# A small scale tile allocated ahead of the split norm operands: their start moves from 0 to 32 modulo 64 bytes

## The chip, the core and the metric

The kernel runs on one core of a Trainium2 chip. The metric is the device time of one execution, in microseconds (us); it is given as the median of several runs. The engines are TensorE (PE; its weight loads are shown apart as PEld), VectorE (DVE), ScalarE (ACT), GpSimd (POOL) and the DMA queue that SyncE issues (SP).

## What is computed

One decoder layer on 512 tokens of width 1024, in float32: a first feed-forward block, two token mixers side by side (a sparse attention whose keys an indexer selects, and a gated linear recurrence) that are merged through gates, a second feed-forward block, and a gated embedding block. Every block stands between two RMS norms.

```python
def reference(x, p, ...):
    h = x
    h = h + 0.5 * rms_norm(swiglu(rms_norm(h, ffn1_pre_g), w_gate, w_up, w_down), ffn1_post_g)   # width 2816 inside
    proj = rms_norm(h, mix_pre_g) @ w_in           # q, latents, index queries and keys, q/f/i/g of the recurrence, gates
    y_a = dsa_branch(...)                          # index scores, top 128 keys per query, attention of 8 heads
    y_b = rms_norm(hgrn2_chunkwise(...), hgrn_norm_g) * silu(g_h)
    merged = sigmoid(gate_a + b) * (y_a @ w_br_a) + sigmoid(gate_b + b) * (y_b @ w_br_b)
    h = h + rms_norm(merged @ w_out, mix_post_g)
    h = h + 0.5 * rms_norm(swiglu(rms_norm(h, ffn2_pre_g), ...), ffn2_post_g)
    return h + rms_norm(sigmoid(rms_norm(h, ple_pre_g) @ w_ple_gate) * (p @ w_ple_proj), ple_post_g)
```

## The kernel before

Activations lie feature-major: a tile of 128 partitions holds 128 features, and 512 tokens run along the free dimension; 1024 features are eight such tiles (index k). A product is made of three matmuls for each step of the contraction, because both operands are split into a high and a low part of a reduced float32 type: weight high by data high, weight low by data high, weight high by data low (`mm3_step`, the matmul of line 239). So a product of 1024 features and 512 tokens is 24 matmuls of 512 columns.

The split data lie in three pairs of tiles:

- `hg_hi` and `hg_lo`, [128, 8, 512] each: h times the gain of the next norm, in parts. They are written by ScalarE (line 283) and VectorE (line 284), and are the data of the gate and up products of both feed-forward blocks, of nearly all of the mixers' products, and of the last block's. In the merge they hold the two branches' results. Where a result is wanted token-major (the values, lines 623 to 625; the latents; the last block) they are the stationary operand and the weight is the moving one.
- `hid_hi` and `hid_lo`: the hidden layer of a feed-forward block, the data of its down products.
- `m_hi` and `m_lo`: the merged branches, the data of w_out's product.

A weight comes by DMA into one of three `raw` tiles, 512 KB at a time, is split by ScalarE (line 163) and VectorE or GpSimd (line 165) into one of six `w` tiles, and is then the stationary operand. `R` holds the norm's scale per token, spread over the partitions; it is multiplied onto a product when VectorE takes it out of PSUM (`scaled`, line 360). `r`, [128, 4], holds the same scale with one token per partition.

Outside the mixers the program's text sets the order, block by block, and at a block's end the last product runs in halves of the tokens (256 columns) beside the norms. In the mixers a table (`PLAN`) says which steps of the scores, the selection, the attention and the recurrence go out behind each product. Each engine takes its instructions in order.

Where tiles lie is settled by the order of allocation. The pools const, keep, wpool and tmp are stacked, and every tile is rounded up to 32 bytes of a partition. `hg_hi`, `hg_lo`, `R` and `r` are the four tiles of keep, in that order, allocated at the end of `consts` (lines 130 to 133). `r` is 16 bytes long and takes 32, so all that follows keep begins 32 bytes past a multiple of 64.

Of the kernel before, what the change touches and what calls it, by code (L numbers as in the profile page):

```python
# [14 lines left out]
P = 128  # L15
# [31 lines left out]
BANKS = {"mm": 2, "pl": 2, "hg": 2, "pt": 1, "po": 1}  # L47
# where a block ends: how many tiles of its last product run in halves of the tokens; for each half, how many matrix
# products go out at the most before the norm's two steps, and how many of the residual's tiles GpSimd adds
TURN = {  # L50
# [3 lines left out]
}  # L54
# the first weights of a block, with * for those whose low part GpSimd takes
FIRST = {"mix": "---*", "ffn2": "*---", "proj": "---", "ple": "-*--*--*"}
# the products of the mixers in order, and the steps of the scores, of the selection, of the attention and of the
# recurrence that go out behind each; * for a product whose weight's low part GpSimd takes
PLAN = (
# [11 lines left out]
class Layer:  # L71
# [27 lines left out]
    def consts(self):  # L99
# [28 lines left out]
        nc.vector.tensor_scalar_add(self.lbn, self.lb, -1.0)  # L128

        self.hg_hi = self.keep.tile([P, KT, NT], F32R, name="hg_hi")  # L130
        self.hg_lo = self.keep.tile([P, KT, NT], F32R, name="hg_lo")
        self.R = self.keep.tile([P, NT], F32, name="R")
        self.r = self.keep.tile([P, 4], F32, name="r")

    def bias_vector(self):
        """The relative bias less its last bucket's, over the scale, for the distances 255 to -128; each head's
        vector is laid out P times, so that a read with rows of BVEC - 1 shifts it by one each."""
        nc, c = self.nc, self.const
        onehot = self.t(BVEC)[:32]
        nc.sync.dma_start(onehot, self.a["onehot"])  # L140
        rel = c.tile([32, HEADS], F32, name="rel")
        nc.sync.dma_start(rel, self.a["rel_bias"])
        far = c.tile([HEADS, 1], F32, name="far")
        nc.sync.dma_start(far, self.a["rel_far"])
        ps = self.bank("pl")
        nc.tensor.matmul(ps[:HEADS, :BVEC], rel, onehot, start=True, stop=True)
        bv = self.t(BVEC)[:HEADS]
        nc.vector.tensor_scalar(bv, ps[:HEADS, :BVEC], far, 1.0 / ATT_SCALE, op0=OP.subtract, op1=OP.mult)
        nc.sync.dma_start(self.bias_d, bv.unsqueeze(1).to_broadcast([HEADS, P, BVEC]))
# [21 lines left out]
    def first_weights(self, name, srcs, n, own=()):  # L171
        """The first weights of a block, the last of them in tiles of the block's own."""
        own = [None] * (len(srcs) - len(own)) + list(own)
        flags = self.first[name]
        return [self.weight(src, n, w, self.nc.gpsimd if next(flags) == "*" else None) for src, w in zip(srcs, own)]

    def weight(self, src, n, w=None, eng=None):
        """One group of a weight: [128, n] raw to its high and low parts."""
        raw = self.raw_tile()
# [9 lines left out]
    def bank(self, tag=None):  # L189
        """A bank of PSUM; outside the mixers the products go round all but those of the norms."""  # L190
        if tag is None:
# [3 lines left out]
    def mm3(self, ps, w, hi, lo, n, cols, c0=0):  # L195
        """ps = w^T x over n tiles of the contraction, from the parts of both."""
        self.mm3s([(ps, w)], hi, lo, n, cols, c0)

    def mm3s(self, outs, hi, lo, n, cols, c0=0):
        """The same for several pairs of a result and a weight, side by side along the contraction."""  # L200
        for k in range(n):
# [21 lines left out]
    def power(self, out, ss, n, *ds):  # L223
        """out = (ss/d + eps)^-1/2"""
        nc = self.nc
# [6 lines left out]
    def issue_after(self, later, earlier):  # L232
        """An order of two instructions of one engine."""
        self.tc.add_manual_dep(later.ins, earlier.ins.name, mybir.DependencyInfo(
            mybir.DependencyClass.NoSync, mybir.DependencyReason.DATA), reason="order of issue")

    def matmul(self, *args, **kw):
        """A product of the main stream, after the ones that ask to go ahead of it."""
        i = self.nc.tensor.matmul(*args, **kw)  # L239
# [7 lines left out]
    def rms(self, acc, cols, r, spread=True, waits=None):  # L247
        """r[token] = (sum(acc)/D + eps)^-1/2 for the tokens of cols; returns it spread over a PSUM tile."""
        nc = self.nc
# [17 lines left out]
    def square_sum(self, acc, src, first, eng):  # L267
        """acc (+)= src^2"""
        nc = self.nc
# [9 lines left out]
    def prenorm_tile(self, k, gname, acc, cols):  # L279
        """h[k] times its gain, in parts; its squares go to acc."""  # L280
        nc = self.nc
# [13 lines left out]
    def start(self, *srcs):  # L295
        """The input and its norm's operands, with the first weights between them; returns the weights."""
        nc = self.nc
# [27 lines left out]
    def residual(self, y, acc, g, nxt, turn, spill=None):  # L325
        """For each half of the tokens: h += g * y / rms(y), and the next norm's operands."""
        nc = self.nc
# [16 lines left out]
    def last_product(self, product, y, acc, g, nxt, turn, spill=None):  # L344
        """The last product of a block: its second half of the tokens runs beside the first half's norms."""
        split = KT - turn[0]
# [10 lines left out]
    def scaled(self, ps, cols=FULL):  # L357
        """The norm's scale on a product, feature-major."""
        t = self.t(cols.stop - cols.start)
# [68 lines left out]

# [1 line left out]

# [19 lines left out]
    def kv_product(self, k, ps, i, ws):  # L450
        """Step k of the contraction of the latents, the index keys and the index weights of token tile i."""
        tok = slice(i * P, (i + 1) * P)
# [6 lines left out]
    def kv_tile(self, i, ps):  # L459
        """Tokens of tile i: the normed latents and index keys, and the index weights, token-major."""  # L460
        nc = self.nc
# [25 lines left out]
    def stacked(self, q, o, t0):  # L487
        """The queries from token t0 of one head of a pair: the high part and the low part, on half of the partitions each."""
        nc = self.nc
# [7 lines left out]
    def dots(self, m, q):  # L497
        """The index scores of heads 2m and 2m + 1, added for the query tiles past the first. A head's queries are
        stacked in both parts on the partitions, so that one pass takes them against one part of the keys."""
        nc = self.nc  # L500
# [21 lines left out]
    def topk(self, qt):  # L522
        """Each query's scores to a mask: 0 for its best TOPK keys, MASKED for the others."""
        nc = self.nc
# [10 lines left out]
    def attention(self, hd):  # L535
        """A head over its own keys, which lie on the partitions twice, against its queries in both parts."""
        nc = self.nc
# [49 lines left out]
    def head_keys(self, m):  # L587
        """The keys of the heads 2m and 2m + 1 from the latents."""
        nc = self.nc
# [15 lines left out]
    def head_values(self):  # L605
        """The values of all heads from the latents, token-major."""
        nc = self.nc
# [23 lines left out]
    def forget(self, ps, hd):  # L631
        """k = 1 - f, and the sums of log f from the start of each chunk."""
        nc = self.nc
# [153 lines left out]
    def mixers(self):  # L787
# [58 lines left out]
        for step, n_dots, n_top, n_att, n_hg in PLAN:  # L846
# [19 lines left out]
            for j, (g, n) in enumerate(((dots, n_dots), (top, n_top), (att, n_att), (hg, n_hg))):  # L866
                run(g, n)
                done[j] += n
            # a query tile's selection comes after all scores, and before its attention
            assert done[0] >= 8 or not done[1]  # L870
# [10 lines left out]
    def merge(self, pool):  # L881
        """The two branches through their gates, w_out, and the residual."""
        nc, a = self.nc, self.a
# [17 lines left out]

        # the first branch runs ahead, for it is ready before the other
        for i in range(KT + LEAD):
# [23 lines left out]
    def ple_proj(self, pool):  # L927
        """The other product of the last block, token-major, which waits for nothing: it fills the end of the first block."""
        nc, a = self.nc, self.a
# [12 lines left out]
    def tok_mm3s(self, outs, w, hi, lo):  # L942
        """For each of several results, some columns of a token tile of x^T w."""
        n = len(w)
# [7 lines left out]
    def ple(self, pp, y, pool):  # L952
        """The last block, token-major: its norm's sums lie along the rows, and a token tile ends by itself."""
        nc, a = self.nc, self.a
# [80 lines left out]
def _square(w, m_tiles):  # L1035
    """[K, M] to [M/128, 128, K]: for each tile of columns, all of the contraction with 128 rows a step."""
    k, m = w.shape
# [63 lines left out]
```

## Time and profile before

| | |
|---|---|
| median of 3 runs | 1270.4 us (1266.41 to 1270.44) |
| span of the profiled execution | 1267.0 us (no other time of it is recorded) |
| PE busy | 1246.2 us, 98% |
| VectorE, ScalarE, GpSimd busy | 56%, 42%, 23% |
| matmuls in the trace | 6263 |
| granted TensorE clock | full but for single slices |

PE's busy time counts matmuls that overlap, so the length of one matmul is no measure of its cost. What one adds is the distance from its start to the next one's start; it is read from the timeline, or from a piece of the chain of work that ended last, where so many matmuls in a row take so long.

### The profile page before, as it was taken

The page shows a single profiled execution, that of the slowest core. Times are in us where ns is not written, and L with a number is a line of the kernel's source. Part 1 is how long each engine was busy: PE and PEld are TensorE (multiplying, and loading weights), DVE is VectorE, ACT ScalarE, POOL GpSimd, SP SyncE. Part 2 cuts the span into 40 slices and gives each one's busy share as a digit, 9 for nine tenths or more (in the row PEclk, how much of TensorE's full clock was granted, in tenths as well). Part 3 has the DMA queues.
Part 4 walks back from the last instruction along what each step waited for, and adds up shares of the span by engine and source line. Part 5 has one row for each costly group of instructions (what it writes and reads, how often), then busy time and mean ns, then how long its engine had stood idle before and what let it go on. Part 6 is the DMA issues. An engine that isn't in the chain of part 4 may idle for free.

```text
span 1267.0 us, 16616 instructions
## 1 busy us (share of the span) xinstructions
PE 1246.2 (98%) x6263; PEld 1032.4 (81%) x6263; DVE 707.8 (56%) x1252; ACT 530.6 (42%) x905; POOL 297.4 (23%) x348
## 2 busy tenths in 40 slices
PE   7999999999999999999999999989999999999997
PEld 6888788888898887888888777988888888888976
DVE  7543225344348659997677558295432444444286
ACT  6432223223246455565757554364322322222263
POOL 3000000000045203636757622360000000000374
PEclk9999999999999999999999999999999999999999
DMA  6433354332335402323222245223323323332141
GB/s 221 132 85 99 84 109 125 105 107 80 89 118 172 149 22 84 129 96 113 68 71 68 92 143 193 73 84 101 116 87 96 98 85 100 100 94 77 64 150 67
DMA packets 45576, 131.29 MB, mean 104 GB/s; under 512 B 5144, under 2 KB 10424, under 8 KB 45496
## 3 DMA queue, kind: packets, MB, share of 16 engines
q1 hardware_dynamic: 45496, 130.24, 33.6%
q8 instruction: 49, 0.80, 0.3%
q14 instruction: 31, 0.25, 0.1%
HBM read 118.16 MB, written 12.06 MB: 103 GB/s over the span
## 4 chain that ended last, share of the span: by engine, by line
PE 86%; DVE 8%; DMA 2%; ACT 2%; issue 1%; POOL 0%; SPq 0%; DVEq 0%; POOLq 0%; ACTq 0%
PE mm L239 35%; PE pl L239 21%; PE po L239 10%; PE pt L239 9%; DVE hg_lo L284 2%; PE po L581 2%; PE hg L705 1%; DVE h L338 1%; DMA g<-gate_d 1%; DVE z L336 1%; DVE w L165 1%; PE pt L577 1%; PE pl L560 1%; PE hg L764 1%; PE mm L625 1%
## 5 line engine op out<-in xcount | busy, mean ns | idle before, releaser
L163 ACT ACTIVATE w<-raw 128x1024 fp32r<-128x1024 f32 (+5 forms) x205 | 208.5, 1021 | 400.2 <-PE mm L239 116.1
L239 PE MATMUL mm<-hg_hi,w 128*128 128x512 f32 (+1 forms) x1104 | 346.2, 392 | 0.4 <-DVE small L569 0.4
L165 DVE TENSOR_TENSOR w<-raw,w 128x1024 fp32r<-128x1024 f32 (+5 forms) x189 | 227.8, 1209 | 109.9 <-ACT w L163 109.9
L239 PEld LDWEIGHTS mm<-hg_hi,w 128*128 128x128 f32 x1104 | 203.5, 188 | 44.5 <-DVE w L165 0.7
L277 POOL TENSOR_TENSOR acc<-acc,sq 128x256 f32<-128x256 f32 x78 | 67.9, 876 | 697.0 <-ACT sq L276 695.6
L239 PE MATMUL mm<-hg_lo,w 128*128 128x512 f32 (+1 forms) x552 | 215.1, 391 | 1.3 <-DVE hg_lo L284 1.3
L239 PE MATMUL pl<-hg_hi,w 128*128 128x512 f32 (+1 forms) x592 | 176.3, 381 | 5.2 <-ACT w L163 5.2
L239 PEld LDWEIGHTS pl<-hg_hi,w 128*128 128x128 f32 x592 | 108.2, 190 | 27.7 <-ACT w L163 5.2
L239 PEld LDWEIGHTS mm<-hg_lo,w 128*128 128x128 f32 x552 | 103.4, 188 | 23.6 <-DVE hg_lo L284 1.5
L239 PE MATMUL pl<-hg_lo,w 128*128 128x512 f32 (+1 forms) x296 | 111.4, 380 | 0.7 <-DVE hg_lo L284 0.7
L239 PE MATMUL pt<-hg_hi,w 128*128 128x512 f32 (+1 forms) x256 | 80.7, 395 | 0.8 <-ACT w L163 0.8
L360 DVE TENSOR_TENSOR t<-mm,R 128x512 f32<-128x512 f32 (+1 forms) x44 | 29.1, 662 | 89.7 <-PE mm L239 69.3
L239 PE MATMUL pl<-hid_hi,w 128*128 128x512 f32 (+1 forms) x290 | 79.0, 359 | 0.0
L239 PE MATMUL po<-hg_hi,w 128*128 128x512 f32 (+1 forms) x256 | 78.7, 388 | 0.0
L239 PE MATMUL mm<-hid_hi,w 128*128 128x512 f32 (+1 forms) x278 | 75.3, 357 | 0.0
L239 PEld LDWEIGHTS pl<-hg_lo,w 128*128 128x128 f32 x296 | 55.7, 189 | 12.2 <-DVE hg_lo L284 1.0
L239 PEld LDWEIGHTS pt<-hg_hi,w 128*128 128x128 f32 x256 | 48.1, 191 | 13.4 <-ACT w L163 1.3
L239 PEld LDWEIGHTS pl<-hid_hi,w 128*128 128x128 f32 x290 | 51.7, 189 | 8.1
L239 PEld LDWEIGHTS po<-hg_hi,w 128*128 128x128 f32 x256 | 47.5, 188 | 10.9
L239 PEld LDWEIGHTS mm<-hid_hi,w 128*128 128x128 f32 x278 | 49.6, 189 | 7.7
L360 DVE TENSOR_TENSOR t<-pl,R 128x512 f32<-128x512 f32 (+1 forms) x30 | 20.1, 671 | 63.6 <-PE pl L239 63.5
L239 PE MATMUL pt<-hg_lo,w 128*128 128x512 f32 (+1 forms) x128 | 50.8, 397 | 2.0 <-DVE hg_lo L284 1.8
(300 smaller groups left out, 2139.2 us busy)
## 6 DMA issues: line engine op xcount, KB each, us to landing
raw<-ffn_w_gate SPq DMA_DIRECT2D x43, 512.0 KB, 3.6
raw<-ffn_w_up SPq DMA_DIRECT2D x43, 512.0 KB, 3.6
raw<-ffn_w_down SPq DMA_DIRECT2D x32, 448.0 KB, 3.3
raw<-ffn_w_down SPq DMA_DIRECT2D x16, 512.0 KB, 3.5
raw<-w_gates SPq DMA_DIRECT2D x16, 512.0 KB, 3.5
gate_d<-t SPq DMA_DIRECT2D x16, 256.0 KB, 2.0
raw<-w_br SPq DMA_DIRECT2D x8, 512.0 KB, 3.3
raw<-w_out SPq DMA_DIRECT2D x8, 512.0 KB, 3.9
```

The source lines that it names most:

```text
L163: hi = nc.scalar.activation(w[:, 0, c], raw[:, c], AF.Copy)
L165: lo = eng.tensor_tensor(w[:, 1, c], raw[:, c], w[:, 0, c].bitcast(F32), op=OP.subtract)
L239: i = self.nc.tensor.matmul(*args, **kw)
L277: eng.tensor_tensor(acc[:, c:c + 256], acc[:, c:c + 256], sq, op=OP.add)
L284: lo = nc.vector.scalar_tensor_tensor(self.hg_lo[:, k, cols], self.h[:, k, cols], g, self.hg_hi[:, k, cols].bitcast(F32), op0=OP.mult, op1 ...
L336: nc.vector.scalar_tensor_tensor(z, y[:, k, c], g[:, k:k + 1], bc, op0=OP.mult, op1=OP.mult)
L338: eng.tensor_tensor(self.h[:, k, c], self.h[:, k, c], z, op=OP.add)
L360: self.nc.vector.tensor_tensor(t, ps, self.R[:, cols], op=OP.mult)
L560: nc.tensor.matmul(pl, st[:, tok], kh[:, part, :nk], start=(part == 0), stop=(part == 1))
L577: nc.tensor.transpose(pt[:, k], lg[:, k], self.ident)
L581: nc.tensor.matmul(po[rows, tok], self.vh[:, kt, hd * IDX:(hd + 1) * IDX], at[:, kt * P:(kt + 1) * P], start=(kt == 0), stop=(kt == qt))
L625: nc.tensor.matmul(ps, self.hg_lo[:, k, tok], w[:, 0, c], start=False, stop=(k == KT - 1))
```

## The change

`r` is allocated ahead of `hg_hi` instead of behind `R`.

```diff
@@ consts @@
         nc.vector.tensor_scalar_add(self.lbn, self.lb, -1.0)
 
+        self.r = self.keep.tile([P, 4], F32, name="r")
         self.hg_hi = self.keep.tile([P, KT, NT], F32R, name="hg_hi")
         self.hg_lo = self.keep.tile([P, KT, NT], F32R, name="hg_lo")
         self.R = self.keep.tile([P, NT], F32, name="R")
-        self.r = self.keep.tile([P, 4], F32, name="r")
```

Comments and docstrings go as well; no other line of code differs. The built programs have the same instructions on each engine, row by row in the same order. What differs is four addresses (bytes in a partition):

| tile | before | modulo 64 | after | modulo 64 |
|---|---|---|---|---|
| hg_hi | 18304 | 0 | 18336 | 32 |
| hg_lo | 34688 | 0 | 34720 | 32 |
| R | 51072 | 0 | 51104 | 32 |
| r | 53120 | 0 | 18304 | 0 |
| w (six tiles from 65440 on, 8192 apart) | | 32 | the same | 32 |
| hid_hi, m_hi; hid_lo, m_lo | 164512; 180896 | 32 | the same | 32 |
| ckvT (the latents) | 154528 | 32 | the same | 32 |

Inside these tiles every operand of a matmul starts a multiple of 64 bytes from the tile's start (the 256-column halves, the 128-column weights and the eight steps of k are 1024, 512 and 2048 bytes apart), so the tile's residue is the operand's; the one exception is the latents' weight, whose columns come 200 to a step.

## Rows read from the trace of the kernel before

**Rows 1.** Page, busy time of each engine, and the granted clock in 40 slices.
```profile
PE 1246.2 (98%) x6263; PEld 1032.4 (81%) x6263; DVE 707.8 (56%) x1252; ACT 530.6 (42%) x905; POOL 297.4 (23%) x348
...
PEclk9999999999999999999999999999999999999999
```

**Rows 2.** Page, the chain that ended last, by engine.
```profile
PE 86%; DVE 8%; DMA 2%; ACT 2%; issue 1%; POOL 0%; SPq 0%; DVEq 0%; POOLq 0%; ACTq 0%
```

**Rows 3.** Pieces of that chain in the first feed-forward block: start, us, what.
```profile
57.39 5.60 PE mm L239 x24
...
118.53 5.44 PE po L239 x24
...
253.63 4.76 PE mm L239 x21
...
268.75 5.60 PE pl L239 x24
```

**Rows 4.** Timeline of PE, a gate product: start, us, engine, line, operation.
```profile
74.73 0.63 PE L239 MATMUL pl<-hg_hi,w 128*128 128x512 f32 x2
75.19 0.40 PE L239 MATMUL pl<-hg_lo,w 128*128 128x512 f32 x1
75.43 0.63 PE L239 MATMUL pl<-hg_hi,w 128*128 128x512 f32 x2
```

**Rows 5.** Timeline of PE, a down product.
```profile
118.37 0.61 PE L239 MATMUL po<-hid_hi,w 128*128 128x512 f32 x2
118.83 0.39 PE L239 MATMUL po<-hid_lo,w 128*128 128x512 f32 x1
119.05 0.61 PE L239 MATMUL po<-hid_hi,w 128*128 128x512 f32 x2
```

**Rows 6.** Groups by line and shape, matmuls of 512 columns with hg, a selection.
```profile
L239 PE MATMUL mm<-hg_hi,w 128*128 128x512 f32 x1040 | 334.7, 399 | 0.4 <-DVE small L569 0.4
...
L239 PE MATMUL po<-hg_lo,w 128*128 128x512 f32 x120 | 47.5, 395 | 0.0
...
L623 PE MATMUL mm<-w,hg_hi 128*128 128x512 f32 x32 | 12.7, 397 | 0.0
...
L239 PE MATMUL pl<-w_ple,hg_lo 128*128 128x512 f32 x6 | 2.4, 394 | 0.0
```

**Rows 7.** Chain, pieces of 256 columns: hid in halves, m, then hg in halves.
```profile
365.65 2.52 PE pt L239 x21
...
805.03 2.88 PE mm L239 x24
...
855.72 2.48 PE mm L239 x21
```

**Rows 8.** Stretches: length, then busy us of PE, PEld, DVE, ACT, POOL; clock, DMA.
```profile
50.00:100.00 50.00, 50.00 (x216) 40.27 (x215) 22.06 (x26) 14.70 (x18) 0.00 (x0) 1.00 0.32 95
100.00:150.00 50.00, 50.00 (x219) 40.49 (x218) 13.53 (x13) 14.06 (x18) 0.00 (x0) 1.00 0.34 97
...
500.00:550.00 50.00, 50.00 (x262) 40.64 (x261) 47.76 (x116) 25.93 (x38) 25.96 (x34) 1.00 0.35 116
550.00:600.00 50.00, 50.00 (x268) 41.66 (x267) 43.47 (x104) 28.53 (x49) 25.45 (x25) 1.00 0.31 100
600.00:650.00 50.00, 50.00 (x296) 40.46 (x297) 33.85 (x99) 35.07 (x73) 36.29 (x48) 1.00 0.21 65
```

**Rows 9.** A stretch as before, instructions that write or read hg_hi alone: PE, PEld.
```profile
500.00:600.00 100.00, 71.75 (x224) 41.18 (x223) 0.00 (x0) 0.00 (x0) 1.00 0.33 108
```

**Rows 10.** Chain, pieces in the mixers: the values of the heads, the wait for VectorE, later products.
```profile
468.63 1.39 PE mm L613 x6
...
470.89 0.72 ACT lg L511 x2
...
490.30 1.15 DVE w L165
491.52 3.98 PE mm L239 x16
...
568.68 5.60 PE mm L239 x24
```

**Rows 11.** Chain, pieces in the merge.
```profile
761.87 5.39 DMA g<-gate_d
...
790.38 2.56 DMA g<-gate_d
...
797.32 0.64 ACT m_hi L186
797.96 0.04 issue
798.00 0.73 PE pt L239 x2
```

**Rows 12.** Chain, pieces at the end: second half's norm, then the last products.
```profile
1225.89 0.46 PE hg L261 x4
...
1241.52 2.87 DVE hg_lo L284 x2
1244.39 0.04 issue
1244.44 2.37 PE mm L239 x9
```

## The prediction, made before the changed kernel ran

> **What bounds the kernel now.** The page comes first: PE is busy for 98% of the span at the full granted clock [rows 1], and 86% of the chain that ended last is PE [rows 2]. So the time is, nearly everywhere, the number of matmuls times the distance between their starts, and the question is whether that distance depends on where the operands lie. The durations of single matmuls don't tell (they overlap); the chain's pieces do. Within one block, with the same weight tiles, the same engines and the same clock, a product of 24 matmuls takes 5.60 us where the data are hg, and 5.44 us where they are hid [rows 3]. That is 233.3 ns a matmul against 226.7. The timeline names the operands: three matmuls with hg take 75.43 - 74.73 = 0.70 us, three with hid 119.05 - 118.37 = 0.68 us [rows 4, 5]. Groups of seven steps agree (4.76 us for 21 with hid, again 226.7 ns [rows 3]). Of the split operands in these rows, hg is the one that starts at 0 modulo 64; weights and hid start at 32.
>
> **The change part by part.** No instruction is added, removed or moved, and no wait. `r` stays at residue 0, and its operations are a few of 128 columns; nothing for them. What is left is 32 bytes on hg and R.
>
> R and the writes of hg: VectorE, ScalarE and GpSimd read or write hg and R at the new address. I take nothing for it; VectorE is no bound in the feed-forward blocks (22.06 busy of 50 us [rows 8]), which covers even a tenth more on each of its operations there. In the mixers that cover is thin, and it returns among the rivals.
>
> Matmuls of 512 columns with hg: the reduced-type groups are eight with hg as data, from x1040 to x120, 3024 in all, and nine with hg as stationary operand, from x32 to x6, 264 in all [rows 6]; 3288 together. If all of them go from 233.3 to 226.7 ns, each gives 6.7 ns, and all give 21.9 us. How much of it reaches the end differs by stage:
>
> - First block: 44 gate and up products, 1056 matmuls. The first two products start with the input's arrival, so I leave out their 48. 1008 x 6.67 ns = 6.7 us, all on the path, since the chain there is nothing but such pieces [rows 3].
> - Second block: 40 products of 512 columns (the first four run in halves), 960 x 6.67 ns = 6.4 us.
> - Mixers: 38 products, 912 matmuls. A run of 24 takes 5.60 us here too [rows 10], so the full gain is 6.1 us. But the nearest row of another pair of operands that both start at 32, the heads' values with the latents, shows 1.39 us for six, 231.7 ns [rows 10], among much other work. By that row the gain is only 1.6 ns each, 1.5 us. The down products' row is a cleaner match for these long runs, so I lean to it: 5.0 us. From 470.9 to 491.5 us the chain runs through ScalarE and VectorE while PE is kept busy, and PE then waits for VectorE [rows 10]; in those 20.6 us PE has at most 88 matmuls of 233.3 ns, and would only reach that wait sooner, by some 0.5 us. That leaves 4.5 us (bounds 1.0 and 6.1).
> - Merge: 192 matmuls, 1.3 us. But there the chain runs through the gates' loads and VectorE to m_hi, for which PE waits [rows 11]: PE sooner means that it waits longer. I take 0 (bounds 0 and 1.3).
> - Last block: 168 matmuls. From 1225.9 to 1244.4 us the chain lies on VectorE [rows 12], and the gain under it is lost. At 233.3 ns each, 79 of the 168 fit into those 18.5 us; the other 89 give 0.6 us.
>
> Matmuls of 256 columns with hg are the other way round: 21 take 2.48 us with hg and 2.52 us with hid, and m has 2.88 us for 24, 120 ns as hid [rows 7]. So a matmul of 256 columns would cost 2 ns more. There are 336 of them (288 with hg as data, 48 in the last block), 0.7 us if all are on the path; some stand in waits at a block's start, so 0.5 us of loss. The latents' 96 matmuls of 200 columns may lose as much each, 0.2 us at most, within the rounding.
>
> Sum: 6.7 + 4.5 + 0 + 6.4 + 0.6 - 0.5 = 17.7 us. The profiled execution would go from 1267.0 to 1249.3 us. Its span is 3.4 us under the median of the runs and inside their spread, so I put the sum on the median: 1270.4 - 17.7 = 1252.7 us.
>
> **The rivals.** *VectorE takes the gain of the mixers.* From 500 to 600 us VectorE is busy for 47.76 and 43.47 us of 50 each [rows 8]. 224 matmuls read hg_hi there [rows 9], half as many again hg_lo; with these 336 shorter by 6.67 ns each, that stretch would shrink by about 2 us, and VectorE would be near 93% of it, with PE's queue in order behind each of its results; or the products there follow the 231.7 ns of the crowded rows. Then the mixers give 0 to 1 us rather than 4.5: 1256.2 to 1257.2 us. For it: PE already waits once for VectorE at 491 us [rows 10]. Against it: in the same stretch the chain is PE alone after that, so VectorE has some slack.
>
> *The start is not the cause, and nothing changes: 1270.4 us.* Gate and up products also differ from down products in what runs beside them: VectorE is busy for 22.06 us of 50 in a stretch of gate and up products, 13.53 us where down products fill most of it [rows 8]. If contention made the 6.7 ns, moving the tile would do nothing. Against it: from 600 to 650 us VectorE has 33.85 and GpSimd 36.29 us [rows 8], while a run of 24 with VectorE at 43.47 us takes the same 5.60 us [rows 10] as one in the first block; the distance does not follow the load. A dependence on where hg lies in a larger sense (it is the lowest of the big tiles) is not excluded by any row, since no split operand lies beside it at another residue. [...]
>
> *A start in the middle of 64 bytes is the dearer one: slower.* A row of 512 values that starts at 32 touches one stretch of 64 bytes more than one that starts at 0. The place where this shows is the 256-column rows, where hid and m at 32 are slower by 2 ns than hg at 0 [rows 7]. If that is what the start does, and the 6.7 ns at 512 columns come from something else, every matmul with hg pays 2 ns: (3288 + 336) x 1.9 ns = 6.9 us, which gives 1277.3 us. It decides if runs of 24 with hg go above 5.60 us. Against it: then hid would need a second reason to be faster at 512 columns, one that turns round at 256.
>
> *Everything reaches the end.* With the merge's 1.3 us, the mixers' full 6.1 us and no loss at 256 columns, up to 21.9 us: 1248.5 us.
>
> **How the numbers follow.** The forecast, 1250 to 1255 us around 1252.7: 0.72. VectorE takes the mixers' gain: 0.14. Everything reaches the end: 0.05. No change: 0.06. Slower: 0.03. Differences under 0.3% (4 us) can hardly be measured on this kernel. The first three cases are faster by more than that, 0.91; no change 0.06; slower 0.03. The range takes in the first three: from 1246 (the full gain, and a spread of runs of which one in three lay 4 us lower before) to 1259 (no gain in the mixers, and 2 us of spread), which leaves out a tenth.
>
> **What will show it.** In the profile after, a run of 24 with hg in the first block should take 5.44 us and the 1267.0 us span some 17.7 less. In detail: the first down product should begin about 2 us sooner (16 products lie before it, the first two of which wait for the input), the mixers' long runs should read 5.44 to 5.56 us, the 21 of 256 columns at the second block's start 2.52 us, the wait at 491 us should grow by half a microsecond, and m_hi should still be what PE waits for at the end of the merge. Wrong would be: runs of 24 still at 5.60 us (no change), above it (slower), or runs at 5.44 us with new waits of PE for VectorE or weights between them (the gain given back).

## The result and the profile after

The kernel before took 1269.99 us in the runs beside the changed one (1266.41 to 1270.44), the changed kernel 1254.14 us (1252.45 to 1255.33): a ratio of 0.988, 95% interval 0.9866 to 0.9893. That is 15.9 us between the medians. The profiled executions lie 14.3 us apart (spans of 1267.0 and 1252.7 us), and the account below is made on these.

The page of the changed kernel, to be read against [rows 1, 2]: busy time of each engine, the granted clock, and the chain that ended last, by engine.

```profile
span 1252.7 us, 16616 instructions
...
PE 1228.4 (98%) x6263; PEld 1031.5 (82%) x6263; DVE 706.7 (56%) x1252; ACT 530.3 (42%) x905; POOL 297.8 (24%) x348
...
PEclk9999999999999999999999999999999999999999
...
PE 82%; DVE 11%; ACT 3%; DMA 2%; issue 1%; SPq 0%; DVEq 0%; POOLq 0%; POOL 0%; ACTq 0%
```

PE is still busy for 98% of the span, with the same instructions, and has lost 17.8 us of busy time; VectorE, ScalarE and GpSimd work as long as before to within 1.1 us. So the 32 bytes acted on PE alone. What acted is seen in the chain's pieces of the first block (start, us, what), the hg products first and a hid product last:

```profile
51.19 5.44 PE po L239 x24
56.63 5.44 PE mm L239 x24
62.07 5.44 PE pl L239 x24
...
116.47 5.44 PE po L239 x24
```

The 24 matmuls with hg that took 5.60 us [rows 3] take 5.44, the same as those with hid. The timeline of PE in a gate product (compare [rows 4]: 0.70 us for three) has 0.68 us for three starts:

```profile
74.14 0.62 PE L239 MATMUL pl<-hg_hi,w 128*128 128x512 f32 x2
...
74.82 0.62 PE L239 MATMUL pl<-hg_hi,w 128*128 128x512 f32 x2
...
75.50 0.62 PE L239 MATMUL pl<-hg_hi,w 128*128 128x512 f32 x2
```

Where the time went is read by laying the start of the same matmul of both traces side by side. These pieces of the chain after answer to [rows 7, 10, 12]: hid in halves at the end of the first block, a run of 24 in the mixers, m in the merge, hg in halves, the last products.

```profile
359.10 2.52 PE pt L239 x21
...
562.30 5.48 PE mm L239 x24
...
797.09 2.88 PE mm L239 x24
...
847.81 2.52 PE mm L239 x21
...
1230.18 2.33 PE mm L239 x9
```

The lead over the kernel before is 365.65 - 359.10 = 6.55 us at the first, then 568.68 - 562.30 = 6.38, 805.03 - 797.09 = 7.94, 855.72 - 847.81 = 7.91, and 1244.44 - 1230.18 = 14.26 us at the last. So both feed-forward blocks give 6.3 to 6.6 us each, and the 440 us between them only 1.4 us together. Finer: at the mixers' start 1.3 us are lost, the mixers themselves (430 to 746 us) give 2.6, the merge 0.1.

| stage | forecast, us | measured, us |
|---|---|---|
| first feed-forward block | 6.7 | 6.55 |
| mixers' start | 0 | -1.3 |
| mixers | 4.5 | 2.6 |
| merge | 0 | 0.1 |
| second feed-forward block | 6.4 | 6.3 |
| last block | 0.6 | 0.1 |
| 256 columns | -0.5 | inside the stages |
| sum | 17.7 | 14.35 (spans: 14.3) |

### The profile page after: what moved, and what is told of

The parts are those of the page before. It is cut to its first block, busy times and chain, and to the rows that moved or that the text cites. A ratio compares the mean times of both kernels' runs of the same rounds, so it can differ in the third digit from the quotient of the medians.

```text
span 1252.7 us, 16616 instructions
## 1 busy us (share of the span) xinstructions
PE 1228.4 (98%) x6263; PEld 1031.5 (82%) x6263; DVE 706.7 (56%) x1252; ACT 530.3 (42%) x905; POOL 297.8 (24%) x348
## 3 DMA queue, kind: packets, MB, share of 16 engines
HBM read 118.16 MB, written 12.06 MB: 104 GB/s over the span
## 4 chain that ended last, share of the span: by engine, by line
PE 82%; DVE 11%; ACT 3%; DMA 2%; issue 1%; SPq 0%; DVEq 0%; POOLq 0%; POOL 0%; ACTq 0%
PE mm L239 33%; PE pl L239 21%; PE po L239 10%; PE pt L239 9%; DVE hg_lo L284 2%; PE po L581 2%; DVE w L165 2%; DVE h L338 1%; DMA g<-gate_d 1%; DVE z L336 1%; PE hg L705 1%; PE pt L577 1%; DVE sc L532 1%; PE pl L560 1%; PE hg L764 1%
## 5 line engine op out<-in xcount | busy, mean ns | idle before, releaser
L239 PE MATMUL mm<-hg_hi,w 128*128 128x512 f32 (+1 forms) x1104 | 340.8, 387 | 0.8 <-DVE small L569 0.8
L239 PE MATMUL mm<-hg_lo,w 128*128 128x512 f32 (+1 forms) x552 | 212.5, 387 | 1.2 <-DVE hg_lo L284 1.2
L239 PE MATMUL pl<-hid_lo,w 128*128 128x512 f32 (+1 forms) x145 | 52.0, 359 | 0.0
```

## The experiments

Two questions were open. Why does the start of hg matter: because its residue modulo 64 is that of the weights (A), because residue 32 is good by itself (B), or for another reason that the address brings along (C)? And what became of the gain in the mixers: lost to interruptions by other matmuls (D), or to VectorE, GpSimd and traffic (E)?

The runs e1 to e5 and e8 have PE's instructions in the order of the changed kernel; only addresses differ. The table behind them gathers what they measured by the distance that turned out to count.

**e1: everything at 0 modulo 64.** In the kernel before, `r` takes 64 bytes in place of 16, still behind R, so that the weights and hid come to residue 0, where hg already is.

```
-        self.r = self.keep.tile([P, 4], F32, name="r")
+        self.r = self.keep.tile([P, 16], F32, name="r")[:, :4]
```

> hg stays at residue 0 modulo 64, as in the kernel before, and everything behind it (weights, hid, m, the mixers' tiles) moves from 32 to 0, so that both operands of every product have the same residue, 0. Theory A, what counts is that the moving and the stationary operand have the same residue: products of 24 with hg take 5.44 us and of 24 with hid 5.44 us as well, and the time is that of the changed kernel, 1250 to 1257 us. Theory B, a start at 32 is fast by itself and one at 0 slow: 5.60 us with hg and 5.60 us with hid too, 1275 to 1280 us. Theory C, it is the place of hg at the low end and no residue: 5.60 us with hg and 5.44 us with hid, 1270 us.

Measured: 1269.39 us, ratio 0.9996 (0.9987 to 1.0006). The chain's pieces of hg and of hid:

```profile
57.34 5.60 PE mm L239 x24
...
118.47 5.44 PE po L239 x24
```

A and the plain form of B both fall: hg shares its residue modulo 64 with the weights here and is as slow as before, and hid at 0 is as fast as at 32. These are the times that were expected under C, and e2 puts C to the test.

**e2: the weights at 0, and all that lies behind them.** The changed kernel with 32 bytes more behind R. hid, m and the mixers' tiles move along with the weights, so their distance from the weights stays; that of hg does not.

```
-        self.R = self.keep.tile([P, NT], F32, name="R")
+        self.R = self.keep.tile([P, NT + 8], F32, name="R")[:, :NT]
```

> hg at 32 modulo 64, as in the changed kernel, and everything behind it at 0: weights 0, hid 0. Theory A (same residue): hg with the weights is mixed again, 5.60 us for 24, hid is even with them, 5.44 us, and the time is that of the kernel before, 1266 to 1272 us. Theory B (32 is fast by itself): weights and hid at 0 make all products slow, or, if the moving operand alone counts, hg 5.44 us and hid 5.60 us, about 1262 us. Theory C (the 32 bytes gave hg a better place): 5.44 us for both, 1254 us.

Measured: 1269.77 us, ratio 0.9999 (0.999 to 1.0009). hg, then hid:

```profile
56.98 5.60 PE mm L239 x24
...
118.13 5.44 PE po L239 x24
```

hg lies at exactly the address of the changed kernel, 18336, and yet takes 5.60 us. So it isn't the place of hg, and C falls too; moving the weights away from hg undoes the whole gain.

**e3: hid alone moved.** The changed kernel; `offset` makes a view that begins some elements inside a larger tile.

```
+    def offset(self, pool, k, first, name):
+        t = pool.tile([P, k * NT + 16], F32R, name=name)
+        return t[:, first:first + k * NT].rearrange("p (k n) -> p k n", k=k)
...
-        hid_hi = pool.tile([P, 8, NT], F32R, name="hid_hi")
-        hid_lo = pool.tile([P, 8, NT], F32R, name="hid_lo")
+        hid_hi = self.offset(pool, 8, 8, "hid_hi")
+        hid_lo = self.offset(pool, 8, 8, "hid_lo")
```

> The changed kernel with hid alone moved from 32 to 0 modulo 64; hg and the weights stay at 32. Theory A: 24 with hid take 5.60 us instead of 5.44, with hg 5.44 us; 866 matmuls of 512 columns with hid lose 6.67 ns each, 5.8 us, and 378 of 256 columns win 2 to 3 ns each, 1 us; 1257 to 1261 us. Theory C: nothing changes, 1254 us. It also tells whether the cost sits with any tile or with hg alone.

Measured: 1257.96 us, ratio 0.9906 (0.9891 to 0.992). hg, then hid:

```profile
57.25 5.44 PE mm L243 x24
...
117.52 5.57 PE po L243 x24
```

Now hg is fast and hid is slow, in down products whose neighbours on the other engines are those of the fast kernel. So with either tile it is the pair of starts, of the data and of the weights, that counts.

**e4: hg 64 bytes further from the weights.** As in the changed kernel, hg and weights have equal residues modulo 64, but 64 bytes are added between them.

```
-        self.r = self.keep.tile([P, 4], F32, name="r")
+        self.r = self.keep.tile([P, 24], F32, name="r")[:, :4]
...
-        self.R = self.keep.tile([P, NT], F32, name="R")
+        self.R = self.keep.tile([P, NT + 16], F32, name="R")[:, :NT]
```

> The changed kernel with hg 64 bytes further up against the weights: equal modulo 64, but 96 against 32 modulo 128. Theory A with a period of 64 bytes: 5.44 us for 24 with hg, 1250 to 1257 us. A period of 128 bytes or more: 5.60 us or another value for hg, 5.44 us for hid (which keeps its residue modulo 128 against the weights), about 1270 us.

Measured: 1267.81 us (one run). hg, then hid:

```profile
57.74 5.60 PE mm L239 x24
...
118.88 5.44 PE po L239 x24
```

That is the second case against 64. Its place in the list of distances is 192 modulo 256, the same as that of e1.

**e5: starts at 48 and 16 modulo 64.** The changed kernel; hg's views begin at element 4 of their tiles, hid's at element 12.

```
-        self.hg_hi = self.keep.tile([P, KT, NT], F32R, name="hg_hi")
-        self.hg_lo = self.keep.tile([P, KT, NT], F32R, name="hg_lo")
+        self.hg_hi = self.offset(self.keep, KT, 4, "hg_hi")
+        self.hg_lo = self.offset(self.keep, KT, 4, "hg_lo")
...
+        hid_hi = self.offset(pool, 8, 12, "hid_hi")
+        hid_lo = self.offset(pool, 8, 12, "hid_lo")
```

> The changed kernel with hg at 48 and hid at 16 modulo 64, the weights at 32: 16 bytes off to either side. If the residue has to be the same to the byte within 64, both products of 24 take 5.60 us or some value between 5.44 and 5.60, and the time lies at 1265 to 1280 us. If only the half of 64 bytes counts (0 to 31 against 32 to 63), hg at 48 is as fast as at 32, 5.44 us, and hid at 16 slow, 5.60 us: 1257 to 1261 us. [...]

Measured: 1273.01 us (one run); hg 5.58 us for 24, hid 5.57. Both pairs of distances in it, of the high and the low part, are slow.

**e8: hg at 128, hid 4 bytes off.** The changed kernel again. If half of 256 bytes were enough, hg would be fast; if a few bytes off were forgiven, hid would be. `offset` is that of e3, with tiles 64 elements longer in place of 16.

```
-        self.r = self.keep.tile([P, 4], F32, name="r")
+        self.r = self.keep.tile([P, 40], F32, name="r")[:, :4]
...
-        self.R = self.keep.tile([P, NT], F32, name="R")
+        self.R = self.keep.tile([P, NT + 32], F32, name="R")[:, :NT]
...
+        hid_hi = self.offset(pool, 8, 1, "hid_hi")
+        hid_lo = self.offset(pool, 8, 1, "hid_lo")
```

> The runs so far leave theory A only as a distance: even are operands whose starts differ by a multiple of 256 bytes (hg after the change, hid throughout), uneven those 16, 32, 48 or 64 off, though a distance of 64 keeps the residue modulo 64. Here hg lies 128 bytes off a multiple of 256 from the weights, and hid 4 bytes off. If the period is 128 bytes, 24 with hg take 5.44 us; if it is 256, 5.60 us or a value near it, as at 64. If the match has to be exact, 24 with hid take 5.55 to 5.60 us; if some bytes off are forgiven, 5.44 us. The time is 1250 to 1260 us with a period of 128, 1265 to 1275 us with 256.

Measured: 1279.1 us (one run). hg, then hid:

```profile
57.25 5.58 PE mm L243 x24
...
118.91 5.68 PE po L243 x24
```

Neither is fast, and 4 bytes off is the slowest of all. The distances together, as start of the moving operand less start of the weight, modulo 256, with the mean time from start to start of 512-column matmuls in the first block, by the chain's pieces of nine products with hg or two with hid (where the high and the low part lie at two distances, the mean is that of both):

| distance | ns | where |
|---|---|---|
| 0 | 226.7 (in e1 226.9) | hg after; hid before, after, in e1, e2 and e4 |
| 4 | 236.7 | hid in e8 |
| 32 and 96 | 232.3 | hid_hi and hid_lo in e3 |
| 48 and 112 | 232.1 | hid_hi and hid_lo in e5 |
| 128 | 232.4 | hg in e8 |
| 144 and 208 | 232.6 | hg_hi and hg_lo in e5 |
| 192 | 233.4, 233.3 | hg in e1, in e4 |
| 224 | 233.3 | hg before and in e2 |

At distance 0 the weights start at 160 modulo 256 (before, after), at 192 (e1, e2) or at 32 (e4): the distance counts, not the place. hg after lies 47104 = 184 x 256 below the weights and hid 99072 = 387 x 256 above, an odd multiple, so 512 isn't needed. What follows: of the distances tried, alone or in pairs, only a multiple of 256 bytes is fast. The residue modulo 64 that the change speaks of came along with that.

**e6 and e7: interruptions alone.** The kernels before and after, with a matmul of 64 columns behind every sixth of 512 in the gate and up products, 336 of them, where there is little work on the other engines: from 60 to 110 us of the changed kernel VectorE, ScalarE and GpSimd are busy for 20.46, 14.65 and 0 of 50 us (in the mixers see [rows 8]).

```
+            if self.breaks and k % 2:
+                self.matmul(self.spare[:, :64], w[:, 0, c], hi[:, k, :64], start=True, stop=True)
```

> The kernel before with an extra matmul of 64 columns behind every sixth of 512 in the gate and up products of both feed-forward blocks (336 in all; its result is used by nothing). With hg at 0 and weights at 32 there is no settled state to lose: the 512-column matmuls keep their 233 ns on average, and each extra matmul adds its own 60 to 110 ns: 1290 to 1310 us.

> The changed kernel with the same extra matmuls. Theory D (even operands are fast only in an unbroken run: in the mixers after the change each run starts with some ten matmuls at 224 to 236 ns and only then keeps 226.7): runs of six never settle, the 512-column matmuls average 230 to 232 ns, and this kernel is only 3 to 7 us faster than its twin with breaks before the change. Rival E (in the mixers the other engines' traffic slows even operands): there is hardly any traffic in these blocks, so the average stays at 227 ns and the lead over the twin is 13 us in these blocks, 15 us in all.

Measured: 1304.1 and 1297.09 us (one run each), 7.0 us apart instead of 14.3. By e6 an interruption costs 102 ns (1304.1 us against 1269.95 of the kernel before beside it, over 336). Pieces of the chain of before with interruptions: hid in halves in the first block, as in [rows 7], then in the second.

```profile
377.99 2.51 PE mm L242 x21
...
1217.48 2.51 PE pt L242 x21
```

And of after with interruptions:

```profile
377.04 2.51 PE mm L242 x21
...
1210.54 2.51 PE pt L242 x21
```

The lead at the end of the first block is 377.99 - 377.04 = 0.95 us instead of 6.55. In the second block it grows from 5.57 (820.29 - 814.72 us, at the merge's first 24 of 256 columns with m) to 6.94 us, 1.4 instead of 6.3. So interruptions by a matmul of another shape take most of the gain by themselves, in blocks where the other engines have little to do: D holds. From 60.83 us on, eight times six matmuls with their interruption took 12.06 us in e6 and 12.00 in e7, 1.3 ns less for each of 512 columns instead of 6.7. Loads alone don't do it: in that stretch of the changed kernel, from 60 to 110 us, DMA is busy for 0.32 of the time, as much as in the mixers [rows 8], and uninterrupted runs of 24 take 5.44 us. E isn't needed for that loss of speed; what VectorE did take in the mixers is in the next section. The rest of the 7.0 us comes between the blocks: the mixers' own 2.6 us, and some 2 us at their start, to which the section on the hardware returns.

**e9: the latents' gain loaded early.** The changed kernel with the tile `kvg` in the constants, loaded at the start of the program. The tile is 768 = 3 x 256 bytes, so no distance changes.

```
+        self.kvg = self.const.tile([P, KV + IDX], F32, name="kvg")
...
-        self.kvg = pool.tile([P, KV + IDX], F32, name="kvg")
```

> The changed kernel with the gain vector of the latents' norm (kvg) loaded in the first feed-forward block into a tile of its own, instead of at the mixers' start behind the weights; its 768 bytes keep all distances modulo 256. After the change PE waits there 1.76 us for VectorE, which waits 4.8 us for this load. Theory: that wait falls away and the stretch up to the first long runs of the mixers gets 1 to 2 us shorter: 1251.5 to 1253.5 us. Rival: another wait (the scale on the first latents, the second half's norm) ends at about the same time, and nothing is gained: 1253 to 1255 us.

Measured: 1252.88 us, ratio 0.986 (0.9843 to 0.9876). PE's wait for the latents at their transposes is gone, and the second of these begin at 414.13 instead of 415.27 us. PE's instructions keep their order; among the DMA issues that of `tp` moved as well.

**e10 and e11: the two best on one chip.** The changed kernel and e9 again, four runs each.

> The changed kernel once more, on the chip that also runs the next one, so that the two can be compared: 1252 to 1256 us, ratio to the kernel before 0.987 to 0.989.

> The early load of kvg again, beside the changed kernel on one chip. By the first trace it is 1.1 us ahead when the second latents' transposes run (the 1.8 us wait is gone, but the granted clock falls to half for 3.4 us in the middle of products instead of behind the wait): 1 us less than the changed kernel, ratio to the kernel before 0.986 to 0.988; the rival, no difference between the two.

Measured: 1253.86 us (ratio 0.988, 0.9863 to 0.9896) and 1251.61 us (0.9861, 0.9845 to 0.9877). The medians are 2.3 us apart and the intervals overlap: the early load is the fastest version seen here, but its own gain isn't settled.

## Why the prediction was right, and where it wasn't

**The size and the mechanism of the main term.** The step from [rows 3] held: hg's matmuls went from 233.3 to 226.7 ns, all of it on the path in both feed-forward blocks (6.55 and 6.3 us for 6.7 and 6.4). The first down product was to start about 2 us sooner. Its piece of the chain starts at 100.15 instead of 102.19 us, or 2.04. The time, 1254.1 us, lies in the central case of 1250 to 1255. The sum of 17.7 us was too high all the same: the medians lie 15.9 us apart, and the two spans 14.3, which is 3.4 less. Nearly all of that is in the mixers and at their start.

**The reason was too weak.** The prediction took residue 32 modulo 64, equal to that of the weights, for what made hid fast. e1 and e4 keep residues equal and are slow; what fits every run is a multiple of 256 between the two starts. The rows of before could not tell these apart: hid and m happen to lie a multiple of 256 from the weights as well as at the same residue modulo 64. Had the change made the residues equal as e1 or e4 do, the same argument would have forecast the same gain, and next to none would have come. That these 32 bytes also made a multiple of 256 was luck. The rival by which the start is not the cause was refuted by e2 and e3 together: e2 moves the weights under an unmoved hg, e3 moves hid over unmoved weights.

**The mixers' term was mis-sized: 4.5 us expected, 2.6 measured.** The step that went wrong is the choice between two rows. The down products' 226.7 ns was taken for the long runs, and the heads' values' 231.7 ns [rows 10] was kept as the lower bound. The traces show that both are right, for different places in one run. The changed kernel's timeline of PE, behind a matmul of 64 columns:

```profile
504.27 0.49 PE L705 MATMUL hg<-hX 128*128 128x64 f32 x3
...
505.12 0.40 PE L625 MATMUL mm<-w,hg_lo 128*128 128x512 f32 x1
...
506.97 0.39 PE L624 MATMUL mm<-w,hg_hi 128*128 128x512 f32 x1
...
509.01 0.39 PE L624 MATMUL mm<-w,hg_hi 128*128 128x512 f32 x1
```

From 505.12 to 506.97 eight matmuls start 231 ns apart on average; from 506.97 to 509.01 nine start 227 ns apart. Through the mixers the second to fifth matmul of a run averages 228 to 232 ns, and the twelfth and later 226.7; before, every place averages some 233. So a short run gains little and a long one nearly all. The chain's pieces between 520 and 600 us show it; after:

```profile
523.89 5.76 PE mm L239 x25
...
535.30 1.82 PE mm L239 x7
...
537.57 1.85 PE mm L239 x8
```

The same three before:

```profile
529.62 5.88 PE mm L239 x25
...
541.25 1.84 PE mm L239 x7
...
543.52 1.87 PE mm L239 x8
```

The run of 25 gained 0.12 us, 4.8 ns each; the runs of 7 and 8 gained 0.02 us, under 3 ns each. A run of 24 read 5.48 us at 562 us, inside the 5.44 to 5.56 that was forecast, but the mixers have some 80 runs of about ten on average. The heads' values' six matmuls of [rows 10] were a whole run of six between other shapes, at a distance that is a multiple of 256 (the latents lie 89088 = 348 x 256 bytes above the weights): not another price, but one not yet settled.

**The rival in which VectorE takes the gain** expected 0 to 1 us from the mixers and was right in a smaller part only. Three of PE's waits for VectorE at the mixers' start and in them, after the change:

```profile
PE pt L479 <- DVE t L473: 1.8, 1, 1.8
...
PE mm L239 <- DVE small L569: 0.8, 1, 0.8
...
PE hg L705 <- DVE hX L690: 0.2, 1, 0.2
```

(who waits for whom, us in total, times, longest). The second row is the wait that [rows 6] show with 0.4 us: it grew by 0.4, where half a microsecond was forecast. The third is new, at 522.6 us. Before, the chain comes back to PE at 491.5 us [rows 10]; after, it stays with VectorE until the third wait ends:

```profile
520.61 0.48 DVE small L531
...
521.74 0.60 DVE t L360
...
522.81 1.08 PE hg L705 x8
```

So the slack that the prediction gave VectorE there was smaller than the gain, and from the one wait to the other the path is the work of VectorE and ScalarE, not PE's. Its price can be read with the starts of the same matmuls of both traces side by side. From 430 to 746 us the steps from one matmul of 512 columns with hg to the next gave 3.5 us, these two waits took 0.38 us each, and all other steps lost 0.2 together: 2.6 us. So of the 5.0 us that were expected before any wait some 3.3 came, as the short runs never settle, and VectorE took 0.8 instead of 0.5. The first row is new too, at the mixers' start, and belongs to the loss of 1.3 us there. No step of the prediction had that; it took the gain of the first block as carried on whole.

**The smaller terms.** The merge gave 0.1 us for 0: PE's first waits for m_hi (0.6 us in total before, 1.1 after) took up what it gained, as said. hg in halves of 256 columns went from 2.48 us for 21 [rows 7] to 2.52, as forecast: at 256 columns distance 0 is the slower one, 120 ns against 118. The last block gave 0.1 us for 0.6. What it gained before the second half's norm, 0.5 us, went into PE's wait for VectorE there, as forecast. But the 89 matmuls behind it that were to give 0.6 us are 33: of the 168, 64 start before 1225.9 us, which the subtraction left out, and 71 in the stretch to 1244.4. The 33 would give 0.2 us at 6.7 ns each, and the 48 of 256 columns behind the wait take 0.1 back. That R and the writes of hg cost nothing holds: VectorE is busy for 706.7 us, 707.8 before.

## What to carry to other kernels

For products of the reduced float32 type with long rows, look at the time from start to start of the same matmul with different operands (durations overlap, 399 ns for starts 233.3 ns apart [rows 3, 6], and don't give it), and compare the distance between the moving and the stationary start modulo 256 bytes; a small tile allocated ahead of large ones shifts all of them. Keep such matmuls in long runs, since here the whole gain came only after some ten of one shape (228 to 232 ns for the second to fifth of a run in the mixers, 226.7 from the twelfth on). And when two operands differ in one residue, try a second distance before naming the rule: what they share may be more than the residue that one looked at.

## What the runs showed of the hardware that was not expected

**The distance between the operands.** At 512 columns the time from start to start follows the distance between the data and the weight: 226.7 ns with hg in the changed kernel, 233.3 in e2, where hg lies at the same address and the weights lie 32 bytes further (1254.1 and 1269.8 us). Where the two meet no run shows. Why 256 bytes, why 4 bytes off is dearest (236.7 ns), and why the order turns round at 256 columns (120 ns at distance 0, 118 before) was not tried.

**Settling.** In the changed kernel's mixers the first ten or so matmuls after one of another shape follow a recurring pattern of 224 to 236 ns even at distance 0, where those of the first block, of one shape throughout, start 226 to 227 ns apart. What makes it is open.

**A stretch at half the clock, at another place in each kernel.** Before, after, in e6, e7 and e9, PE runs at a granted clock of about 0.50 for a few microseconds at the mixers' start: 3.4 us before and after. In e1 and e3 it seems to last longer: 24 matmuls of 200 columns that take 4.55 us in e4 and 4.56 in e9 take 5.45 and 5.44 there. It is too short to show in the 40 slices of a page. The stretches, with length, busy times by engine, clock and DMA; before, then after:

```profile
409.00:412.00 3.00, 3.00 (x16) 3.00 (x16) 1.45 (x6) 0.35 (x1) 1.41 (x2) 0.50 0.83 208
```

```profile
410.50:413.90 3.40, 3.40 (x18) 3.40 (x17) 1.66 (x8) 1.99 (x7) 0.70 (x1) 0.50 0.02 10
```

Before, PE had waited 1.1 us for GpSimd and 0.6 us for ScalarE; about a microsecond later the clock fell, and PE worked slowly on products that had to be there only by 415.5 us, when the load of kvg landed and the latents went on. After, the same two waits (0.8 and 0.6 us) came at 399 to 401 us and the clock stayed; it fell behind the next wait, 1.8 us for the latents, and the slow stretch lay on products on the path. Six of them, before and after:

```profile
417.73 0.73 PE pl L239 x6
```

```profile
411.57 1.33 PE pl L239 x6
```

The lead at the latents' first transposes is 415.54 - 408.92 = 6.62 us, and 429.96 - 424.73 = 5.23 us at the last: that is where the 1.3 us of the table went. In e9, with no wait for the latents, the clock fell at 402.4 us, right behind the first two waits. In the pair with interruptions it was the other way round, before in the first fence, after in the second:

```profile
434.00:437.20 3.20, 3.20 (x18) 3.20 (x17) 1.62 (x8) 1.79 (x6) 0.70 (x1) 0.51 0.06 23
```

```profile
424.80:428.00 3.20, 3.20 (x18) 3.20 (x18) 1.84 (x8) 0.72 (x3) 1.41 (x2) 0.53 0.76 236
```

There e6 has it behind its wait for the latents (which ends at 432.6 us) and e7 right behind its first two waits, with no wait for the latents at all, and e7's lead grows by 2 us over this place, from 432.65 - 431.70 = 0.95 to 448.67 - 445.75 = 2.92 us. So a microsecond or two of a comparison can hang on where these stretches fall. In all five the stretch lies behind a wait of PE; whether a wait brings it on, and which, is not settled by these rows.
